# Branch products in another order, one set of weight slots, and a norm in four steps: a hybrid encoder layer

## The chip, the core and the metric

The kernel runs on one core of a Trainium2 chip. The metric is the device time of one execution in microseconds (us), the median of several runs. A core has five engines with a queue each: TensorE (PE in the profile: matrix products, with a separate queue of weight loads, PEld), VectorE (DVE), ScalarE (ACT), GpSimd (POOL) and SyncE (SP), which here issues every DMA. The engines run side by side and wait for one another by semaphores; each works off its own queue in order.

## The reference

One layer over x of 1024 tokens by 1024 features, all in float32. The shift, scale and gate of each of the three sublayers come from a conditioning vector.

```
x += 0.5 * g1 * SwiGLU1(mod1(RMSNorm(x)))                       # first feed-forward, width 2816
h  = mod2(RMSNorm(x))
x += g2 * W_out( sigmoid(gA) * W_A(FoX(h)) + sigmoid(gB) * W_B(DSA(h)) )
x += 0.5 * g3 * SwiGLU2(mod3(RMSNorm(x)))                       # second feed-forward
```

FoX and DSA are two attentions of 8 heads each, 512 features wide; their outputs are the two branches. Each goes through its own matrix (512 by 1024), is multiplied by a sigmoid gate, and the sum of both goes through W_out (1024 by 1024).

## The kernel before

**Arithmetic.** Activations lie with features on the 128 partitions and tokens along the free axis, in two halves of 512 tokens. Every float32 operand is split into a high and a low part (ACT makes the high one by a copy, DVE the low one by a subtraction), and a product is three matmuls: high x high, high x low, low x high. So each weight tile costs one operation on ACT and one on DVE before PE can use it; `wh` and `wl` in the profile are these parts, `wr` and `a` the raw weights as loaded.

**Feed-forwards.** Both use a two-by-two scheme with seven products instead of eight. `Operands` makes the seven right-hand operands from the normalized input: b11, b21 from the first token half, b22, t1, t2, t3, t4 from both halves. `UpPair` does the up products of one pair of feature blocks in 14 steps (seven operands, two matrices); there are 11 pairs. A product is 12 matmuls of 128x512. The first four steps need only the first token half, so the pairs at the head run these first, while the second half is made ready. `UpPair.load1` loads the two raw weights of a pair for each of two matrices (four half tiles), `load2` the other four, `sum32` and `sum14` form weight sums on DVE. `Down` runs seven passes (0 to 6) of 11 steps, each step two splits and 12 matmuls; at the end of a pass DVE adds the four results to the residual.

**Norm between first feed-forward and mixer.** `stats` takes the mean square of a token half (four tiny matmuls against a column of ones, `nacc`, and a reciprocal root in 12 small DVE operations), `norm_spread` broadcasts the factors by four matmuls, and `norm_apply` then makes the mixer's input block by block: DVE multiplies (`nt`), ACT scales and shifts, ACT copies the high part (`h`), DVE subtracts for the low part. For the first token half this is put into pass 5 of `Down`, four blocks at step 6 and four at step 8 (line 2088). For the second half it comes after pass 6. `first(tk)` projects a block of 128 tokens onto 432 columns, in 24 matmuls; it needs only the first half for tk 0 to 3.

**Branches and output.** `Branches.first` (beside the attention) does two of the eight output blocks of the first branch. `Branches.rest` does the others: it goes through the output blocks d two at a time, for each the products of the first and then of the second branch (line 1783), then gates, adds and splits the results. The gated values are `gr`, loaded from DRAM and overwritten. The merged operand m of the first token half goes to the pool h0b, that of the second half ("m" in the profile) to "common". `mixer_out` multiplies by W_out in 16 steps and does beside it the loads of x, the statistics and the first operands of the second feed-forward.

**Slots.** Tiles come from named homes: "h0" and "h1" (16 tiles each), "c" (the pool "common", 52 tiles in the first feed-forward and 41 from the branches on), and "g". In the last stage "g" holds raw weights of the branches, of W_out and of the up pairs; it is the class `Pairs`, which takes over the six tiles of 128x1024 of an older pool, two each under the tags wr, wh and wl, and cuts every one into two halves. A new tile takes the next tag in rotation and has to wait for one of the two buffers of that tag.

**Order.** The kernel doesn't issue instructions as written. `Plan` collects them as tasks in the written order, with a cost for each, and `flush` (line 292) lists them: at each step it takes over all engines the task that can start first, ties going to the one written first, with slots taken from those that have come free. The result is the fixed order of each engine's queue. The first feed-forward up to the mixer's first projection is one plan (to line 2132), and branches, output and second feed-forward are another (line 2280).

Of the kernel before, what the change touches and what calls it, by code (L numbers as in the profile page):

```python
# [9 lines left out]
F32 = mybir.dt.float32  # L10
# [56 lines left out]
class Pairs:  # L67


    def __init__(self, p, tags):  # L70
        self.p, self.tags, self.n, self.rest = p, tags, 0, None
# [73 lines left out]
class LateTile(View):  # L145
# [8 lines left out]
    def real(self):  # L154
        if self.t is None:
            kw = self.kw
            if self.pool.own and kw.get("tag"):
                if self.slot is None:
                    free = self.pool.plan.slots(self)
                    free.sort()  # L160
                    self.slot = free.pop(0)[1]
                    free.append(((free[-1][0] if free else 0.0) + 1.0, self.slot))
                kw = dict(kw, tag=f"{kw['tag']}{self.slot}", bufs=1)
            self.t = self.pool.p.tile(self.full, self.dt, **kw)
        return self.t
# [25 lines left out]
class Plan:  # L191
# [6 lines left out]
    def __init__(self, tc):  # L198
        self.tc, self.on, self.tasks, self.behind = tc, False, [], 0
        self.free = {e: 0.0 for e in self.ENGINES}  # L200
        self.wire, self.done, self.spare, self.window = 0.0, {}, 10, 200
        self.kept, self.wanted = {}, []
# [59 lines left out]
    def close(self):  # L262

        self.on = False
        for x in self.kept.values():
            if x.slot is not None:
                self.slots(x).append((x.end, x.slot))
# [24 lines left out]
    def flush(self, keep=()):  # L292
# [38 lines left out]
        while len(order) < len(tasks):  # L331
# [40 lines left out]
            for x in t.tiles:  # L372
                x.uses -= 1
                x.end = max(getattr(x, "end", 0.0), end)
                if not x.uses and x.slot is not None:
                    self.slots(x).append((x.end, x.slot))
# [994 lines left out]
class Operands:  # L1371
# [37 lines left out]
    def second(self):  # L1409
# [5 lines left out]
        t2, t3 = [], []  # L1415
# [310 lines left out]
class Branches:  # L1726
# [40 lines left out]
    def rest(self, pt1):  # L1767
        k, nc = self.k, self.k.nc
        m = [[None] * 8, [None] * 8]
        for d0 in range(0, 8, 2):  # L1770
            if d0 == 0:
                w = [lambda c, i=i: part8(self.w[i], c) for i in range(2)]
                for hf in range(2):
                    for pr in range(4):
                        t, a, b = k.h_tile(0, F32), t512(k, F32R, "yh"), t512(k, F32R, "yl")
                        nc.sync.dma_start(t, k.d_y[1][pr][:, hf * H:hf * H + H])
                        split(k, a, b, t)
                        self.y[hf].append((a, b))
            else:
                w = [[k.wq.split(k.wq.raw(self.wbr[d0 + i], j, "c" if d0 == 2 else "g")) for j in range(2)] for i in range(2)]  # L1780
                w = [lambda c, i=i, w=w: part4(w[i], c) for i in range(2)]
            ps = {}
            for br in range(d0 == 0, 2):
                for i in range(2):
                    for hf in range(2):
                        ps[br, i, hf] = pt1()
                        self.product(ps[br, i, hf], w[i], br, hf)
            for i in range(2):
                for hf in range(2):
                    sl, t = slice(hf * H, hf * H + H), []  # L1790
                    for br in range(2):
                        if (br, i, hf) in ps:
                            g = t512(k, name="gr")
                            nc.sync.dma_start(g, k.d_gate[br * 8 + d0 + i, :, sl])
                            self.gated(g, ps[br, i, hf])
                            t.append(g)
                        else:
                            t.append(self.t[i][:, sl])
                    nc.vector.tensor_add(t[1], t[1], t[0])
                    a, b = (k.h_tile(0) if hf == 0 else t512(k, F32R, "m") for _ in range(2))  # L1800
                    split(k, a, b, t[1])
                    m[hf][d0 + i] = (a, b)
# [93 lines left out]
def layer(tc, xT, c, pos, ada_w, ada_b, ng, inv, w13a, w2a, w_a, w_f, w_q, w_g, fb, fg, dg, wbr, wout, w13b, w2b, out):  # L1896
    with ExitStack() as es:
# [55 lines left out]
        with ExitStack() as ph:  # L1953
# [134 lines left out]
            steps = {(5, 4): [lambda: stats(0)], (5, 6): [lambda: h0(range(4))], (5, 8): [lambda: h0(range(4, 8))]}  # L2088
# [25 lines left out]

            stats(1)
            rb = norm_spread(k, rms[1], bank)
            first(0)
# [105 lines left out]
        with ExitStack() as ph:  # L2223
# [3 lines left out]
            k.homes = {"h0": (hp[0], "h", 16), "h1": (hp[1], "h", 16), "g": (Pairs(w2, (("wr", 2), ("wh", 2), ("wl", 2))), "g", 12),  # L2227
# [118 lines left out]
```

## Time and profile before

| | |
|---|---|
| median of 3 runs | 2262.19 us (2261.89 to 2266.63) |
| the profiled execution | 2265.69 us |
| its span, first to last instruction | 2264.0 us |
| instructions | 31118 |
| PE busy | 2184.9 us |
| DVE busy | 1800.8 us |
| ACT busy | 1097.6 us |
| mean granted clock of PE | 0.988 |
| DMA packets | 315.89 MB |

Times in the profile are microseconds from the start of the span. Almost every instruction is issued from one line of `flush`, so that all rows bear its number, L386, and groups are told apart by the names of their tiles: `b<-h,wh` is a matmul that writes a bank b of the result memory from operand h with weight wh. Behind a row in the timeline, brackets give the idle time of the engine just before it and what ended it. The granted clock is 1.00 at full rate and 0.50 at half.

### The profile page before, as it was taken

Reading aid. Unit: us, or ns where it says so; the run is one execution under the profiler, and the core shown is the slowest. Engines: PE = TensorE matmul, PEld = TensorE weight load, DVE = VectorE, ACT = ScalarE, POOL = GpSimd, SP = SyncE. Lnnn points to the kernel's source line nnn. Section 1 sums busy time; section 2 is a strip of 40 time slices with the busy share of each in tenths; the row PEclk is TensorE's granted clock in tenths of the full one; section 3 lists DMA queues with packets and bytes.
Section 4 is the critical chain, followed back from the end, with each engine's and each line's share of the span. In section 5 each row is a group of like instructions: output and inputs, shape, how many; then the busy total and the mean of one; then the engine's idle time right before and its main releaser. Section 6 shows DMA issues by size and latency. Waiting matters only on the chain.

```text
span 2264.0 us, 31118 instructions
## 1 busy us (share of the span) xinstructions
PE 2184.9 (97%) x10508; PEld 1802.6 (80%) x10508; DVE 1800.8 (80%) x3387; ACT 1097.6 (48%) x1994; POOL 271.9 (12%) x257
## 2 busy tenths in 40 slices
PE   7999999999999999999899999999999999999999
PEld 5777788787878989987677787787778888888887
DVE  7998987889785488888888877768978877769765
ACT  5432332344463475778777777423533333334443
POOL 0000000000010223222555443000000000000000
PEclk9999999999999999999999999999999999999999
DMA  9234554497321313333332212658123442258520
GB/s 332 84 111 161 170 168 135 149 362 253 112 86 48 120 62 115 117 121 109 122 105 92 72 56 87 239 192 278 61 92 125 145 132 94 94 182 318 167 76 38
DMA packets 186269, 315.89 MB, mean 140 GB/s; under 512 B 27238, under 2 KB 51814, under 8 KB 186108
## 3 DMA queue, kind: packets, MB, share of 16 engines
q1 hardware_dynamic: 186108, 313.89, 41.2%
q8 instruction: 83, 1.36, 0.2%
q14 instruction: 78, 0.64, 0.1%
HBM read 237.53 MB, written 76.28 MB: 139 GB/s over the span
## 4 chain that ended last, share of the span: by engine, by line
PE 44%; DVE 3%; ACT 3%; issue 1%; DMA 1%; SPq 0%; DVEq 0%; ACTq 0%; POOL 0%; POOLq 0%
PE b L386 33%; PE py L386 6%; PE p L386 2%; PE pt L386 2%; ACT pth L386 1%; ACT pr L386 1%; DMA wr<-d_y 0%; DVE wl L386 0%; ACT qs L386 0%; DMA wr<-in_w_g 0%; DVE ptl L386 0%; DMA mraw<-in_ada_w 0%; DVE macc L386 0%; DVE qs L386 0%; DVE xb L386 0%
## 5 line engine op out<-in xcount | busy, mean ns | idle before, releaser
L386 PE MATMUL b<-h,wh 128*128 128x512 f32 x2688 | 851.1, 399 | 15.1 <-ACT wh L386 8.9
L386 PEld LDWEIGHTS b<-h,wh 128*128 128x128 f32 x2688 | 509.1, 190 | 140.6 <-ACT wh L386 13.4
L386 PE MATMUL b<-h,wl 128*128 128x512 f32 x1344 | 529.0, 396 | 2.0 <-DVE wl L386 2.0
L386 ACT ACTIVATE wh<-wr 128x512 fp32r<-128x512 f32 (+2 forms) x366 | 245.3, 678 | 470.4 <-PE b L386 338.4
L386 PEld LDWEIGHTS b<-h,wl 128*128 128x128 f32 x1344 | 255.0, 190 | 63.6 <-DVE wl L386 3.5
L386 DVE TENSOR_TENSOR z<-b,z 128x512 f32<-128x512 f32 x308 | 207.4, 684 | 76.0 <-PE b L386 74.3
L386 PE MATMUL b<-wl,wh 128*128 128x512 f32 x616 | 240.4, 390 | 5.5 <-DVE wl L386 5.5
L386 PE MATMUL b<-wh 128*128 128x512 f32 x616 | 238.7, 390 | 1.9 <-ACT wh L386 1.2
L386 PE MATMUL b<-wh,wl 128*128 128x512 f32 x616 | 239.7, 389 | 0.0
L386 DVE TENSOR_TENSOR wl<-wr,wh 128x512 fp32r<-128x512 f32 x308 | 204.1, 683 | 36.0 <-ACT wh L386 35.9
L386 ACT ACTIVATE wh<-a 128x512 fp32r<-128x512 f32 x132 | 83.3, 631 | 192.6 <-PE b L386 169.0
L386 POOL TENSOR_TENSOR wl<-wr,wh 128x1024 fp32r<-128x1024 f32 (+2 forms) x58 | 123.7, 2137 | 299.3 <-ACT wh L386 299.3
L386 DVE TENSOR_TENSOR wl<-a,wh 128x512 fp32r<-128x512 f32 x132 | 91.4, 692 | 75.4 <-ACT wh L386 75.4
L386 PEld LDWEIGHTS b<-wl,wh 128*128 128x128 f32 x616 | 115.6, 188 | 31.5 <-DVE wl L386 7.5
L386 PEld LDWEIGHTS b<-wh 128*128 128x128 f32 x616 | 115.6, 188 | 27.1 <-ACT wh L386 1.7
L386 PEld LDWEIGHTS b<-wh,wl 128*128 128x128 f32 x616 | 115.5, 188 | 24.1 <-DVE wl L386 0.2
L386 DVE TENSOR_TENSOR z<-z 128x512 f32<-128x512 f32 x176 | 119.5, 691 | 10.9 <-ACT wh L386 0.5
L386 PE MATMUL pj<-wh,h 128*128 128x384 f32 (+1 forms) x512 | 126.4, 325 | 0.1
L386 POOL TENSOR_SCALAR pr<-pr,mn 128x128 f32<-128x128 f32 (+7 forms) x128 | 101.6, 806 | 154.8 <-DVE mn L386 123.2
L386 DVE TENSOR_TENSOR wl<-g,wh 128x512 fp32r<-128x512 f32 x154 | 106.7, 695 | 0.0
L386 PE MATMUL p<-kst,qs 128*128 128x512 f32 (+5 forms) x384 | 104.0, 363 | 1.8 <-DVE qs L386 0.7
L386 PE MATMUL py<-h,wh 128*128 128x512 f32 x288 | 102.5, 409 | 1.6 <-DVE qs L386 1.4
(298 smaller groups left out, 3806.3 us busy)
## 6 DMA issues: line engine op xcount, KB each, us to landing
d_g<-z SPq DMA_DIRECT2D x154, 256.0 KB
g<-d_g SPq DMA_DIRECT2D x154, 256.0 KB
mraw<-in_ada_w SPq DMA_DIRECT2D x144, 256.0 KB
wr<-in_w13a SPq DMA_DIRECT2D x112, 256.0 KB
wr<-in_w13b SPq DMA_DIRECT2D x88, 256.0 KB
wr<-in_w_g SPq DMA_DIRECT2D x32, 512.0 KB
a<-in_w2a SPq DMA_DIRECT2D x44, 256.0 KB
a<-in_w2b SPq DMA_DIRECT2D x44, 256.0 KB
```

Of the source, the lines that this page charges most:

```text
L386: getattr(getattr(self.tc.nc, e), t.op)(*map(real, t.a), **{n: real(v) for n, v in t.kw.items()})
```

## The change

It has four parts.

- `Pairs` no longer rotates over tags. Its six tiles are one set, and a new one takes any that is free. `Plan.merge` joins the lists of free slots, and `Plan.release` gives a slot back to the joint list; these are steps of the planner in Python and issue no instruction.
- `Operands.second`, used in both feed-forwards, keeps two of its sums in place of old tiles of x instead of four new tiles. t1's difference is now made first, with t2; t3's is made just before its conversion; the subtraction for t4 moves behind t1's conversion.
- `Branches.rest` does all remaining products of the first branch (d = 2 to 7, both token halves), keeping the twelve gated results in "common", and then all eight blocks of the second branch. The loads of the second branch's values come after the first block of the first branch. Weights of the first branch go to "c", of the second to "g". The merged operand of the second token half goes to h1.
- The norm of the first token half moves from two steps in pass 5 to four steps of two blocks each in pass 6, and the first projection block is written ahead of the statistics of the second token half.

```diff
@@ class Pairs
-            tag, bufs = self.tags[self.n % len(self.tags)]
-            self.n += 1
-            t = self.p.tile([128, T], dt, tag=tag, name=name, bufs=bufs)
+            t = self.p.tile([128, T], dt, name=name, **self.kw)
@@ class Plan
+    def release(self, x):
+        key, n = self.merged.get(x.key, (x.key, 0))
+        self.done[key].append((x.end, n + x.slot))
+
+    def merge(self, pool, tags):
+        n, to = 0, (pool, "any")
+        self.done[to] = []
+        for tag, bufs in tags:
+            self.done[to] += [(t, n + i) for t, i in self.done.get((pool, tag), [(0.0, i) for i in range(bufs)])]
+            self.merged[pool, tag] = to, n
+            n += bufs
@@ Operands.second
         def sums(c):
-            t3.append(t512(k, name="t3"))
             t2.append(t512(k, name="t2"))
-            self.any.tensor_sub(t3[c], x[c + 4][1], x[c][1])
-            self.any.tensor_add(t2[c], x[c][0], t3[c])
+            self.any.tensor_sub(x[c][0], x[c][1], x[c][0])
+            self.any.tensor_sub(t2[c], x[c + 4][1], x[c][0])
             self.pair("t2", t2[c], self.shift(c + 4), "h1")
...
         for c in range(4):
-            self.pair("t3", t3[c], d[:, c:c + 1], "h1")
+            self.any.tensor_sub(x[c][1], x[c + 4][1], x[c][1])
+            self.pair("t3", x[c][1], d[:, c:c + 1], "h1")
+        yield
+        for c in range(4):
+            self.pair("t1", x[c][0])
         for c in range(4):
             self.any.tensor_sub(x[c + 4][0], x[c + 4][0], t2[c])
-        yield
-        for c in range(4):
-            self.any.tensor_sub(x[c][1], x[c][1], x[c][0])
-            self.pair("t1", x[c][1])
         yield
@@ Branches.rest, the new loops
+        for d in range(2, 8):
+            w = half(d, 0, "c")
+            for hf in range(2):
+                t[d, hf] = gated(0, d, hf, w)
+            if d == 2:
+                for hf in range(2):
+                    for pr in range(4):
+                        y, a, b = k.h_tile(0, F32), t512(k, F32R, "yh"), t512(k, F32R, "yl")
+                        nc.sync.dma_start(y, k.d_y[1][pr][:, hf * H:hf * H + H])
+                        split(k, a, b, y)
+                        self.y[hf].append((a, b))
+        for d in range(8):
+            w = (lambda c: part8(self.w[d], c)) if d < 2 else half(d, 1, "g")
+            for hf in range(2):
+                g = gated(1, d, hf, w)
+                nc.vector.tensor_add(g, g, t[d, hf])
+                a, b = k.h_tile(hf), k.h_tile(hf)
+                split(k, a, b, g)
+                m[hf][d] = (a, b)
@@ layer
-            steps = {(5, 4): [lambda: stats(0)], (5, 6): [lambda: h0(range(4))], (5, 8): [lambda: h0(range(4, 8))]}
+            steps = {(5, 4): [lambda: stats(0)]}
+            steps.update({(6, c): [lambda c=c: h0(range(c, c + 2))] for c in range(0, 8, 2)})
...
+            first(0)
             stats(1)
             rb = norm_spread(k, rms[1], bank)
-            first(0)
             first(1)
```

Here `gated(br, d, hf, w)` does one product, loads its gate and multiplies; `half(d, br, home)` loads and splits the half tile of weights of one branch.

More of the change, by code (lines that the diff above doesn't have):

```diff
@@ L67, with __init__ @@
 class Pairs:
-    def __init__(self, p, tags):
-        self.p, self.tags, self.n, self.rest = p, tags, 0, None
+    def __init__(self, plan, p, tags):
+        self.p, self.rest = p, None
+        self.kw = dict(tag="any", bufs=sum(n for _, n in tags), names=[f"{t}{i}" for t, n in tags for i in range(n)])
+        plan.merge(id(p), tags)
     def tile(self, shape, dt, name, **_):
         if self.rest is None:
-            tag, bufs = self.tags[self.n % len(self.tags)]
-            self.n += 1
-            t = self.p.tile([128, T], dt, tag=tag, name=name, bufs=bufs)
+            t = self.p.tile([128, T], dt, name=name, **self.kw)
             self.rest = t[:, H:T]
@@ L162, in real @@
                     free.append(((free[-1][0] if free else 0.0) + 1.0, self.slot))
-                kw = dict(kw, tag=f"{kw['tag']}{self.slot}", bufs=1)
+                kw = dict(kw, tag=kw["names"][self.slot] if "names" in kw else f"{kw['tag']}{self.slot}", bufs=1)
+                kw.pop("names", None)
             self.t = self.pool.p.tile(self.full, self.dt, **kw)
@@ L266, in close @@
             if x.slot is not None:
-                self.slots(x).append((x.end, x.slot))
+                self.release(x)
         self.kept = {}
@@ L375, in flush @@
                 if not x.uses and x.slot is not None:
-                    self.slots(x).append((x.end, x.slot))
+                    self.release(x)
                     self.kept.pop(id(x), None)
@@ L1769, in rest, with gated @@
         m = [[None] * 8, [None] * 8]
-        for d0 in range(0, 8, 2):
-            if d0 == 0:
-                w = [lambda c, i=i: part8(self.w[i], c) for i in range(2)]
+        t = {(i, hf): self.t[i][:, hf * H:hf * H + H] for i in range(2) for hf in range(2)}
+        def gated(br, d, hf, w):
+            ps = pt1()
+            self.product(ps, w, br, hf)
+            g = t512(k, name="gr")
+            nc.sync.dma_start(g, k.d_gate[br * 8 + d, :, hf * H:hf * H + H])
+            self.gated(g, ps)
+            return g
@@ L1782, in rest @@
[L1782 to L1802, printed above, removed]
+        for d in range(8):
[6 more added lines that the diff above has]
+                m[hf][d] = (a, b)
```

15 lines of the change are left out of this document (6 added, 9 removed).

## The prediction

> **What bounds the kernel now.** I read the page first, then a table of stages, then in each stage TensorE's idle times with the names of what ended them.
>
> ```profile
> PE 2184.9 (97%) x10508; PEld 1802.6 (80%) x10508; DVE 1800.8 (80%) x3387; ACT 1097.6 (48%) x1994; POOL 271.9 (12%) x257
> ```
>
> TensorE (PE) is busy for 2184.9 of 2264.0 us, and no matmul is added or dropped by this change. So all that can be won is idle time of PE, 79.1 us, and time that it spends at a lower clock. The table of stages (columns: busy us of PE, of its weight load, of DVE, ACT, POOL, then granted clock, DMA share, GB/s) shows where that is:
>
> ```profile
> 0.00:350.00 350.00, 327.85 (x1381) 257.85 (x1382) 311.46 (x542) 127.61 (x214) 1.19 (x8) 0.97 0.50 170
> 350.00:725.00 375.00, 366.14 (x1604) 298.51 (x1603) 303.28 (x501) 165.22 (x287) 9.87 (x8) 0.99 0.49 167
> 725.00:1430.00 705.00, 670.52 (x3974) 581.06 (x3973) 554.30 (x1324) 503.30 (x991) 260.89 (x241) 0.99 0.30 99
> 1430.00:1607.00 177.00, 175.08 (x765) 140.41 (x764) 136.46 (x227) 64.81 (x108) 0.00 (x0) 1.00 0.67 227
> 1607.00:1700.00 93.00, 86.30 (x358) 68.68 (x357) 78.60 (x135) 36.96 (x63) 0.00 (x0) 0.94 0.21 73
> ```
>
> The rows are: first FFN's up products, its down passes with the norm into the mixer, projections and attention, branches with output projection, and the head of the second FFN. The change edits code in all but the third. The stage of the branches holds only 1.9 us of idle time. The two that can give something are the norm (640 to 714) and the head of the second FFN (1607 to 1668). PE's timeline has these waits there (start, duration, instruction, and in brackets the idle time before it and who ended it):
>
> ```profile
> 664.23 0.50 PE L386 MATMUL b<-wl,wh 128*128 128x512 f32 x1 [0.22 <-DVE wl L386]
> 669.78 0.47 PE L386 MATMUL b<-wh 128*128 128x512 f32 x1 [0.72 <-DVE nt L386]
> 679.95 0.50 PE L386 MATMUL b<-wl,wh 128*128 128x512 f32 x1 [3.18 <-DVE wl L386]
> 706.15 1.86 PE L386 MATMUL b<-ones_col,nacc 128*128 128x1 f32 x8 [2.33 <-DVE nacc L386]
> ...
> 1640.33 0.51 PE L386 MATMUL b<-h,wl 128*128 128x512 f32 x1 [1.96 <-DVE wl L386]
> 1655.64 1.22 PE L386 MATMUL b<-h,wh 128*128 128x512 f32 x2 [3.46 <-ACT wh L386]
> 1665.06 0.51 PE L386 MATMUL b<-h,wh 128*128 128x512 f32 x1 [0.39 <-DVE z L386]
> 1666.45 0.50 PE L386 MATMUL b<-h,wh 128*128 128x512 f32 x1 [0.89 <-DVE h L386]
> ```
>
> Some waits are followed by a time at half clock. The table in steps of 2 us (same columns; the number behind PE's busy time also counts matmuls cut by the edges):
>
> ```profile
> 678.00:680.00 2.00, 0.05 (x1) 0.05 (x1) 2.00 (x5) 1.23 (x3) 0.00 (x0) 1.00 0.87 316
> ...
> 706.00:708.00 2.00, 1.85 (x9) 1.85 (x9) 0.10 (x1) 0.00 (x0) 0.00 (x0) 0.50 0.12 47
> 712.00:714.00 2.00, 2.00 (x13) 1.93 (x12) 0.00 (x0) 0.53 (x1) 0.00 (x0) 0.82 0.02 6
> ...
> 1640.00:1642.00 2.00, 1.67 (x6) 1.34 (x7) 2.00 (x5) 0.06 (x1) 0.00 (x0) 0.79 0.00 0
> 1642.00:1644.00 2.00, 2.00 (x6) 1.62 (x5) 1.28 (x3) 0.08 (x1) 0.00 (x0) 0.50 0.00 0
> 1644.00:1646.00 2.00, 2.00 (x9) 1.53 (x9) 1.65 (x3) 1.59 (x3) 0.00 (x0) 0.86 0.00 0
> ...
> 1656.00:1658.00 2.00, 2.00 (x6) 1.47 (x6) 1.60 (x3) 0.28 (x1) 0.00 (x0) 0.50 0.94 303
> 1660.00:1662.00 2.00, 2.00 (x7) 1.55 (x6) 0.60 (x1) 1.26 (x3) 0.00 (x0) 0.59 0.00 0
> ```
>
> Time lost there is two us times one minus the clock: 2 x (0.21 + 0.50 + 0.14) = 1.7 us after the wait of 1.96; 2 x (0.50 + 0.50 + 0.41) = 2.8 after that of 3.46 (1658 to 1660 is at 0.50 too); about 3.4 after that of 2.33 (706 to 712 at 0.50, then 0.82). The wait of 3.18 has 1.00 behind it and cost only itself.
>
> **Sum of what is there to win.** Norm: 0.22 + 0.72 + 3.18 + 2.33 = 6.45, and 3.4 of clock: 9.85 us. Head of the second FFN: 1.96 + 3.46 + 0.39 + 0.89 = 6.70, and 1.7 + 2.8: 11.2 us.
>
> **One set of weight slots.** The six half-pairs of "g" were handed out by rotation over wr, wh, wl with two buffers each. Counting the loads in the order of the code (4 tiles in the branches, then output weights, pair 0 between the 14th and the 15th of them, pairs 1 and 2 after), pair 0's second half, pair 1's first and pair 2's second are tiles 19, 22 and 25: all three fall on wh. So pair 2's second half must wait until pair 0 has used its own for the last time, while a slot of wl stands empty. The trace agrees: up to 1610 there are 18 loads of these weights where pairs 0 to 2 ask for 20 (8, 8 and 4), and the chain of waits then shows the missing two, released by the last weight split of pair 0:
>
> ```profile
> wr<-in_w13b SPq DMA_DIRECT2D x18, 256.0 KB
> ...
> 1651.15 0.61 DVE wl L386
> ...
> 1651.78 3.07 DMA wr<-in_w13b
> ...
> 1654.95 0.64 ACT wh L386
> ...
> 1655.64 8.58 PE b L386 x24
> ```
>
> With any free slot the load joins those of about 1600, and two products of 12 matmuls move ahead of the wait at 1638. Two undisturbed stretches give their length (branch products, of the same form, then down passes):
>
> ```profile
> 1475.00:1500.00 25.00, 25.00 (x109) 20.28 (x109) 13.27 (x21) 5.07 (x8) 0.00 (x0) 1.00 0.25 85
> 2100.00:2125.00 25.00, 25.00 (x112) 20.71 (x111) 19.02 (x31) 10.38 (x18) 0.00 (x0) 1.00 0.68 232
> ```
>
> 24 matmuls at 25 us / 109 are 5.5 us. The wait of 3.46 and its 2.8 of clock go. The 1.96 goes too if DVE's weight split at 1639.6 comes at most 5.5 us later: what the two products bring to DVE ahead of it is two splits, an add and a product, 4 x 0.6 = 2.4 us, so it does, with 1.1 us to spare (1639.6 + 2.4 against 1638.3 + 5.5, less 0.7 for the split itself). What is late next is DVE, which holds the operands of the second half:
>
> ```profile
> 1637.18 2.49 DVE L386 TENSOR_TENSOR xb<-xb,t 128x512 f32<-128x512 f32 x4
> 1639.59 0.69 DVE L386 TENSOR_TENSOR wl<-s,wh 128x512 fp32r<-128x512 f32 x1
> ...
> 1647.46 3.09 DVE L386 TENSOR_TENSOR wl<-wr,wh 128x512 fp32r<-128x512 f32 x5
> ```
>
> So I keep a remainder: at best 0, at worst all that DVE ended (1.96 + 0.39 + 0.89 + 1.7 = 4.9), and take 2.5, the middle. Gain 11.2 - 2.5 = 8.7 us.
>
> **Operands made in place.** Before and after, each block of four has 8 subtractions or additions for the sums, 4 for t4 and 4 for the last operand, all of 0.6 us by the rows above (2.49 for four, 3.09 for five). None is added; four for t3 now stand ahead of its conversion and four for t4 go behind t1. Four slots of "common" are freed. Zero in both FFNs, unless the re-planning below says otherwise.
>
> **Norm in four steps.** Now it runs in bursts of four blocks inside pass 5 of 0 to 6 (654 and 667), in which DVE stands still behind ACT:
>
> ```profile
> 654.02 2.47 DVE L386 TENSOR_TENSOR nt<-xc,b 128x512 f32<-128x512 f32 x4
> ...
> 659.05 0.69 DVE L386 TENSOR_TENSOR h<-nt,h 128x512 fp32r<-128x512 f32 x1 [0.68 <-ACT h L386]
> ```
>
> A burst takes DVE 7 us (654.0 to 661.1), so the weight splits come late, and the second burst meets the additions between passes: hence 0.22, 0.72 and 3.18. After, pass 5 has none of this and enters pass 6 with its splits ahead. Pass 6 asks of DVE 22 splits and 16 norm operations of 0.60, 8 additions of 0.66 and 4 square sums of 0.60: 30.5 us, beside 132 matmuls of 25 us / 112 = 29.5 us on PE. That is tight: with four stalls of 0.68 DVE is 33.2 us, 3.7 over. Against it stand the splits done ahead, up to 4 of 11 steps (8 slots, two each), 10.7 us of PE's work. Bounds: 0, and 3.7 with a half clock like 1.7 to 2.8, so about 6; I take 2.5, since an earlier pass end with the same 8 additions shows 0.96:
>
> ```profile
> 610.36 0.50 PE L386 MATMUL b<-wl,wh 128*128 128x512 f32 x1 [0.96 <-DVE wl L386]
> ...
> 713.72 21.61 PE L386 MATMUL b<-wa,h 128*128 128x432 f32 x108
> ```
>
> The 12 matmuls of the first mixer block that filled a hole at 674 go behind the pass: no cost, PE does them either way.
>
> **First mixer block ahead of the statistics.** The four tiny matmuls waited 2.33 us for DVE's last square, with 24 ready matmuls queued behind them on PE. Now those 24 (21.61 / 108 = 0.20 us each in the last row, 4.8 us) cover it; the statistics then come 2.5 us later, and the rest of their chain (7.6 us, from 706.15 to 713.72) has 72 matmuls, 14.4 us, over it. 2.33 and 3.4 go. Norm: 9.85 - 2.5 = 7.35 us.
>
> **Branches.** 28 products, 28 gate loads, 12 weight loads, 8 loads of the second branch's values: the same counts on PE, DVE, ACT and SP. What moves is order. The first product now needs a loaded and split weight instead of the second branch's values:
>
> ```profile
> 1435.02 0.50 PE L386 MATMUL b<-yl,wh 128*128 128x512 f32 x1 [0.91 <-DVE yl L386]
> ...
> 1431.77 0.45 SPq L386 DMA_DIRECT2D d_y<-yt  x1
> ```
>
> That 0.91 goes if the weight is loaded early. If SP issues it only after the last store of the attention at 1431.77, it lands 3.07 later, and with ACT's 0.64 PE waits from 1433.5 to 1435.5, 2 us, and perhaps 1.7 of clock: -0.9 to +2.8. I take 0. The twelve gated tiles fill slots that the merged operand leaves ("m", 16 tiles, goes to h1); these are free once the first branch is done.
>
> **The sum.** 8.7 + 7.35 = 16.05 us off the profiled execution of 2265.69 us, 3.5 above the median of 2262.19. I take the same 16 us off the median: **2246.0 us**.
>
> **The clock rule.** By the Trainium skill (TensorE: Matmul & The Clock Gate, "What's actually happening") the clock halves after at least one idle window of about 3.4 us, and the windows run freely. The rows differ: half clock stands behind waits of 1.96 and 2.33 us, not behind 3.18, so the measurement decides on the length; the free phase fits both. What follows for time is rival D.
>
> **The rivals.**
> A. DVE can't carry the norm in pass 6: the remainder is the 6 us of the bound and 3.5, half a burst, by which the last blocks hold up the first mixer block; 9.5 instead of 2.5. For: 30.5 against 29.5 us. Against: splits ahead. 2253.0 us.
> B. The change doesn't do what it says in the second FFN: the load comes no earlier, since the planner sends it behind others, or DVE ends the same wait: 8.7 less, 2254.7. Against: the slot count above.
> C. A and B: 2261.7, no change.
> D. Half clock falls by phase: with all times moved, two of the remaining waits, such as 3.82 at 227 (below), get it or lose it, 2.8 us each: 2251.6, or 2240.4.
> E. Slower: the order on every engine is a list plan, and the whole first FFN is one plan, so the freed slots shift its loads. DVE is busy for 311 of its first 350 us, and there is a stall already:
>
> ```profile
> 226.94 1.65 PE L386 MATMUL b<-h,wh 128*128 128x512 f32 x3 [3.82 <-ACT wh L386]
> 228.00:230.00 2.00, 2.00 (x6) 1.61 (x5) 2.00 (x4) 0.00 (x0) 0.00 (x0) 0.50 0.67 202
> ```
>
> Such a stall costs 3.82 and, as above, 2.8 of clock: 6.6 us. It decides from the fourth on, which takes 26.4 for the 16 won: **2272.6 us**. Against: DVE's work there is the same.
>
> **Chances.** Forecast 0.45, A 0.15, B 0.10, C 0.04, D 0.08, E 0.18, of which 0.04 are two or three stalls only, no change. A measurement of this kernel can tell about 0.2%, 4.5 us, from nothing: faster 0.78, same 0.08, slower 0.14. Range: all 21 us, 0.9 at the branches and 4 of D's clock give 2236; on the other side it takes in A and B and reaches to C, 2261.
>
> **What would show it.** Right: 20 loads of the up weights before 1610, no DMA in PE's chain there, no idle time before the statistics' matmuls, and clock 1.00 in both places. Wrong: waits for wl inside pass 6 every two steps (A), the two products still behind pair 0 (B), new waits before 300 us (E).

## The result and the profile after

The changed kernel takes 2254.46 us (median of 6 runs, 2250.57 to 2257.17) beside 2266.61 us (median of 6, 2261.89 to 2269.36) of the kernel before: ratio 0.9943, 95% interval 0.9928 to 0.9958, 12 us faster. Measured a second time, with the last four runs below, it was 0.9921 (0.9906 to 0.9936), 17 us. The profiled executions are 2265.69 and 2255.36 us. The forecast of 16 us less lies between the two measurements; the forecast time of 2246.0 us is 8.5 below the result.

The page's first line and the table of stages of the changed kernel, with the same columns and edges as before (its rows bear the line number L400):

```profile
PE 2180.4 (97%) x10508; PEld 1799.2 (80%) x10508; DVE 1798.8 (80%) x3387; ACT 1099.3 (49%) x1994; POOL 273.7 (12%) x257
```

```profile
0.00:350.00 350.00, 325.60 (x1370) 255.43 (x1371) 310.18 (x541) 126.88 (x213) 1.20 (x8) 0.98 0.50 170
350.00:725.00 375.00, 371.96 (x1641) 304.13 (x1641) 304.37 (x506) 168.22 (x290) 10.65 (x8) 1.00 0.50 168
725.00:1430.00 705.00, 669.13 (x3964) 578.77 (x3962) 554.49 (x1325) 501.91 (x988) 261.86 (x241) 0.99 0.30 96
1430.00:1607.00 177.00, 172.10 (x741) 137.92 (x742) 140.38 (x234) 64.56 (x106) 0.00 (x0) 0.99 0.74 247
1607.00:1700.00 93.00, 92.88 (x409) 75.27 (x408) 82.99 (x142) 42.85 (x70) 0.00 (x0) 1.00 0.17 60
```

The work on each engine is the same. In the second row PE's idle time fell from 8.9 to 3.0 us, in the last from 6.7 to 0.1, and its clock there rose from 0.94 to 1.00. In the fourth row it went the other way, 1.9 us idle became 4.9, and in the first 22.2 became 24.4. PE's timeline names what stands behind this: first the end of the norm, where the statistics' matmuls (`ones_col,nacc`) now stand between mixer blocks and wait for nothing, then the two new waits, one at the start of the branches and one at the output projection.

```profile
703.77 2.56 PE L400 MATMUL b<-wa,h 128*128 128x432 f32 x12
706.21 1.05 PE L400 MATMUL b<-ones_col,nacc 128*128 128x1 f32 x8
707.12 3.02 PE L400 MATMUL b<-wa,h 128*128 128x432 f32 x14
...
1432.40 1.20 PE L400 MATMUL b<-h,wh 128*128 128x512 f32 x4 [2.61 <-ACT wh L400]
...
1533.53 0.50 PE L400 MATMUL b<-h,wl 128*128 128x512 f32 x1 [2.50 <-DVE wl L400]
```

Of the eight waits that the prediction listed, 0.2 us is left in the norm and 0.1 at the head of the second feed-forward. In the chain of waits that head is two stretches of PE with a weight split of DVE between them, and no transfer stands in it; and among the DMA issues between 1430 and 1610 there are 23 loads of its up weights, 18 before:

```profile
1599.89 49.17 PE b L400 x219
...
1650.37 0.61 DVE wl L400
...
1651.03 19.16 PE b L400 x82
```

```profile
wr<-in_w13b SPq DMA_DIRECT2D x23, 256.0 KB, 4.7
```

The wait of 2.61 us is the one whose length the prediction worked out for the branches. In the chain of waits a store (SPq) is followed by the load of the first weight, ACT's split and PE; SP's own timeline shows why the load was not earlier, five stores of the attention that wait for the data which DVE makes for them (in both lists: start, duration):

```profile
1427.94 0.45 SPq L400
1428.48 3.16 DMA wr<-in_wbr
1431.72 0.64 ACT wh L400
```

```profile
1412.86 15.53 SPq L400 DMA_DIRECT2D d_y<-yt  x5
1428.48 0.54 SPq L400 DMA_DIRECT2D wr<-in_wbr  x1
```

**One ruler for all runs.** Two profiled executions differ by some us in places that no edit touches, so whole times hide the parts. Four points are easy to find in each trace: the wait of 0.96 at the end of a down pass, the first product of the mixer (`pj`), the last of the attention (`py`), the first of the second feed-forward's down passes. In the changed kernel:

```profile
615.15 0.50 PE L400 MATMUL b<-wl,wh 128*128 128x512 f32 x1 [0.96 <-DVE wl L400]
...
741.21 0.33 PE L400 MATMUL pj<-wh,h 128*128 128x384 f32 x1
...
1429.40 0.39 PE L400 MATMUL py<-h,wl 128*128 128x512 f32 x1
...
2038.81 0.39 PE L400 MATMUL b<-wh 128*128 128x512 f32 x1
```

The starts of these rows cut a trace in four. A is the first feed-forward to its fourth down pass, B the rest of it with the norm and the mixer's first projection, C projections and attention, D branches, output and the up products of the second feed-forward. Behind D come the down passes of the second feed-forward, 210.5 us from their first matmul to the start of their last in every trace. Lengths in us of all profiled executions, named after the parts that each kernel has; the last column is the time lost to half clock within C, two us times one minus the clock over rows of 2 us:

| kernel | A | B | C | D | lost in C |
|---|---|---|---|---|---|
| before | 610.4 | 136.2 | 686.7 | 615.9 | 6.8 |
| slots | 614.6 | 137.7 | 687.4 | 604.1 | 6.9 |
| norm | 614.1 | 126.1 | 687.9 | 615.6 | 8.5 |
| branches | 612.5 | 137.6 | 689.8 | 617.3 | 8.5 |
| operands | 615.2 | 137.9 | 688.8 | 613.6 | 6.8 |
| slots, norm | 612.3 | 126.0 | 686.2 | 605.0 | 5.1 |
| slots, norm, branches | 612.0 | 126.0 | 688.6 | 606.8 | 6.8 |
| slots, norm, operands | 614.3 | 126.1 | 688.4 | 604.7 | 6.8 |
| all (after) | 615.2 | 126.1 | 688.2 | 609.4 | 6.8 |
| all, old start of the branches | 611.7 | 126.1 | 690.4 | 605.2 | 8.5 |
| all, second profile | 613.1 | 126.1 | 692.7 | 607.9 | 12.0 |
| slots, norm, second profile | 613.5 | 126.1 | 686.4 | 604.9 | 5.1 |
| slots, second profile | 613.7 | 136.1 | 689.2 | 604.4 | 8.5 |
| norm, second profile | 609.3 | 126.1 | 688.1 | 615.4 | 8.5 |

### The profile page after: what moved, and what is told of

Its sections match the earlier page's. It is cut to its first block, busy times and chain, and to the rows that moved or that the text cites. A ratio compares the mean times of both kernels' runs of the same rounds, so it can differ in the third digit from the quotient of the medians.

```text
span 2253.6 us, 31135 instructions
## 1 busy us (share of the span) xinstructions
PE 2180.4 (97%) x10508; PEld 1799.2 (80%) x10508; DVE 1798.8 (80%) x3387; ACT 1099.3 (49%) x1994; POOL 273.7 (12%) x257
## 3 DMA queue, kind: packets, MB, share of 16 engines
q8 instruction: 83, 1.36, 0.3%
## 4 chain that ended last, share of the span: by engine, by line
PE 44%; DVE 3%; ACT 2%; DMA 1%; issue 1%; SPq 0%; ACTq 0%; POOL 0%; DVEq 0%; POOLq 0%
PE b L400 33%; PE py L400 7%; PE p L400 2%; PE pt L400 2%; ACT pth L400 1%; DVE gr L400 1%; DVE macc L400 1%; ACT pr L400 1%; ACT qs L400 0%; DMA wr<-in_w_g 0%; DMA wr<-in_wbr 0%; DVE ptl L400 0%; DMA wr<-in_wout 0%; DVE h L400 0%; DVE wl L400 0%
## 5 line engine op out<-in xcount | busy, mean ns | idle before, releaser
L400 PE MATMUL b<-h,wh 128*128 128x512 f32 x2816 | 887.5, 397 | 13.4 <-ACT wh L400 11.4
L400 PEld LDWEIGHTS b<-h,wh 128*128 128x128 f32 x2816 | 530.9, 189 | 143.6 <-ACT wh L400 16.0
L400 PE MATMUL b<-h,wl 128*128 128x512 f32 x1408 | 554.0, 396 | 4.6 <-DVE wl L400 4.5
L400 ACT ACTIVATE wh<-wr 128x512 fp32r<-128x512 f32 (+2 forms) x366 | 245.1, 678 | 448.3 <-PE b L400 315.1
L400 PEld LDWEIGHTS b<-h,wl 128*128 128x128 f32 x1408 | 266.2, 189 | 69.5 <-DVE wl L400 6.8
L400 DVE TENSOR_TENSOR z<-b,z 128x512 f32<-128x512 f32 x308 | 207.9, 687 | 76.6 <-PE b L400 75.0
L400 PE MATMUL b<-wl,wh 128*128 128x512 f32 x616 | 240.6, 391 | 2.1 <-DVE wl L400 1.9
L400 PE MATMUL b<-wh,wl 128*128 128x512 f32 x616 | 240.5, 391 | 0.0
L400 PE MATMUL b<-wh 128*128 128x512 f32 x616 | 238.0, 390 | 1.8 <-ACT wh L400 1.8
L400 DVE TENSOR_TENSOR wl<-wr,wh 128x512 fp32r<-128x512 f32 x308 | 203.8, 686 | 31.1 <-ACT wh L400 31.0
L400 ACT ACTIVATE wh<-a 128x512 fp32r<-128x512 f32 x132 | 83.4, 632 | 190.1 <-PE b L400 169.5
L400 POOL TENSOR_TENSOR wl<-wr,wh 128x1024 fp32r<-128x1024 f32 (+2 forms) x58 | 123.8, 2139 | 307.0 <-ACT wh L400 303.2
L400 DVE TENSOR_TENSOR wl<-a,wh 128x512 fp32r<-128x512 f32 x132 | 91.4, 692 | 74.8 <-ACT wh L400 74.8
L400 PEld LDWEIGHTS b<-wl,wh 128*128 128x128 f32 x616 | 115.9, 188 | 27.4 <-DVE wl L400 3.2
L400 PEld LDWEIGHTS b<-wh 128*128 128x128 f32 x616 | 116.0, 188 | 26.7 <-ACT wh L400 2.3
L400 PEld LDWEIGHTS b<-wh,wl 128*128 128x128 f32 x616 | 116.0, 189 | 24.3 <-DVE wl L400 0.4
L400 DVE TENSOR_TENSOR z<-z 128x512 f32<-128x512 f32 x176 | 119.5, 691 | 9.9 <-ACT z L400 0.3
L400 PE MATMUL pj<-wh,h 128*128 128x384 f32 (+1 forms) x512 | 126.5, 325 | 0.1
L400 POOL TENSOR_SCALAR pr<-pr,mn 128x128 f32<-128x128 f32 (+7 forms) x128 | 102.5, 814 | 154.9 <-DVE mn L400 124.8
L400 DVE TENSOR_TENSOR wl<-g,wh 128x512 fp32r<-128x512 f32 x154 | 106.6, 694 | 0.3 <-ACT wh L400 0.3
L400 PE MATMUL p<-kst,qs 128*128 128x512 f32 (+5 forms) x384 | 104.0, 363 | 1.9 <-DVE qs L400 0.7
L400 ACT ACTIVATE z<-z 128x512 f32<-128x512 f32 x88 | 55.5, 630 | 101.0 <-DVE z L400 99.7
```

Source lines behind the costliest of these rows:

```text
L400: getattr(getattr(self.tc.nc, e), t.op)(*map(real, t.a), **{n: real(v) for n, v in t.kw.items()})
```

## The experiments

**The theory** is that of the prediction: slots and norm each gain at their own place, the other two parts cost little. **The rival** is that the net of 12 us hides a larger gain and a loss made by the branches or the operands, or that the parts work on each other. First each part alone, all on one chip. Rows of PE in the fences of this section are from PE's timeline of the kernel just named.

**Slots alone.** The new `Pairs`, and in the plan `merge` and `release`; all else as before.

```diff
-            tag, bufs = self.tags[self.n % len(self.tags)]
-            t = self.p.tile([128, T], dt, tag=tag, name=name, bufs=bufs)
+            t = self.p.tile([128, T], dt, name=name, **self.kw)
```

> The kernel before with only the one set of weight slots. Theory (each part acts in its own stage, and the parts add up): the late load of the second half of pair 2 goes, with it the waits of 1.96 and 3.46 us and the half clock behind both at the head of the second feed-forward; 8 to 11 us faster, nothing before 1600 us changed. Rival (the gain there needs the slots of the pool common that the other parts free): DVE still ends a wait of 2 us or more near 1640, at most 5 us faster.

Measured: 2257.59 us (12 runs) beside 2266.08, ratio 0.9960 (0.9949 to 0.9972). Of the four waits at the head of the second feed-forward one is left:

```profile
1655.88 0.51 PE L400 MATMUL b<-h,wl 128*128 128x512 f32 x1 [0.48 <-DVE wl L400]
```

D is 604.1 and 604.4 us in its two profiles, against 615.9, 615.6 and 615.4 in the three profiles with the old slots, branches and operands. With the slots and the old branches and operands (four profiles) the mean is 604.6: a gain of 11.0 us. The wait of 2 us or more near 1640 that the rival asked for isn't there.

**Norm alone.** Four steps in pass 6, and the first block ahead of the statistics.

```diff
-            steps = {(5, 4): [lambda: stats(0)], (5, 6): [lambda: h0(range(4))], (5, 8): [lambda: h0(range(4, 8))]}
+            steps = {(5, 4): [lambda: stats(0)]}
+            steps.update({(6, c): [lambda c=c: h0(range(c, c + 2))] for c in range(0, 8, 2)})
...
+            first(0)
             stats(1)
             rb = norm_spread(k, rms[1], bank)
-            first(0)
```

> The kernel before with only the norm in four steps of pass 6 and the first projection block ahead of the statistics. Theory: the four waits between 664 and 706 (6.45 us) and 3.4 us at half clock go; 8 to 10 us faster, and the first 600 us are as before. Rival (the up products of the first feed-forward are in the same plan, and it is this edit that shifts them): some of the 4.8 us that the changed kernel loses before 615 us appear here, so 4 to 6 us faster.

Measured: 2259.62 us (10 runs) beside 2266.08, ratio 0.9970 (0.9959 to 0.9982). No wait is left in the norm; the head of the second feed-forward keeps its four, of which the two long ones are

```profile
1634.48 0.50 PE L386 MATMUL b<-h,wl 128*128 128x512 f32 x1 [1.97 <-DVE wl L386]
1650.08 1.22 PE L386 MATMUL b<-h,wh 128*128 128x512 f32 x2 [3.75 <-ACT wh L386]
```

B is 126.0 or 126.1 us in all nine profiles with this part, 136.1 to 137.9 in the five without it (mean 137.1): 11.0 us gained. The spread on one side only is the half clock, 3.4 us in two of the five and 5.1 in three. With its mean of 4.4 the waits of 6.45 us make 10.9. By the rival, part of the loss before 615 us should appear here; A is 3.7 us longer than before in this profile and 1.1 shorter in the second one, so nothing shows it. The whole time gives less than the stretch, 6.5 us (4.1 to 9.3 by the interval), and in the second measurement 11.5; why it gave less the first time stays open.

**Branches alone.**

```diff
-        for d0 in range(0, 8, 2):
+        for d in range(2, 8):
+            w = half(d, 0, "c")
...
+        for d in range(8):
+            w = (lambda c: part8(self.w[d], c)) if d < 2 else half(d, 1, "g")
```

> The kernel before with only the new order of the branches. Theory: a wait of 2.6 us at the first branch product (its weight is issued behind the last store of the attention) in place of 0.9, and a wait of 2.5 us with 1.7 of half clock early in the output projection, where loads of the modulation weights, let in by freed slots, hold DVE; together 5 to 6 us slower, unless more free slots shorten the head of the second feed-forward. Rival (the second wait comes from the other parts): only 2 us slower.

Measured: 2271.12 us (12 runs) beside 2266.08, ratio 1.0023 (1.0013 to 1.0034), slower. The wait of 0.91 at the start became 2.48, and a second one is new at the output projection:

```profile
1442.64 2.07 PE L386 MATMUL b<-h,wh 128*128 128x512 f32 x4 [2.48 <-ACT wh L386]
...
1544.51 0.50 PE L386 MATMUL b<-h,wl 128*128 128x512 f32 x1 [1.42 <-DVE wl L386]
```

With 1.7 us of half clock behind the first this is 2.48 - 0.91 + 1.7 + 1.42 = 4.7 us. Its profile has only 1.7 us of half clock at the head of the second feed-forward, where the kernel before has 5.1, so that D is only 1.4 us longer than in that profile.

**Operands alone.**

```diff
-            self.any.tensor_sub(t3[c], x[c + 4][1], x[c][1])
-            self.any.tensor_add(t2[c], x[c][0], t3[c])
+            self.any.tensor_sub(x[c][0], x[c][1], x[c][0])
+            self.any.tensor_sub(t2[c], x[c + 4][1], x[c][0])
```

> The kernel before with only the operands made in place. Theory: the four freed slots change the plan of the first feed-forward's up products, waits around 100 us grow from 3.8 to 5.8 and one more of 1.8 near 557; 3 to 5 us slower by 615 us, nothing in the second feed-forward. Rival (those differences are not from the operands): within 1 us of the kernel before at 615 us.

Measured: 2269.98 us (12 runs) beside 2266.08, ratio 1.0018 (1.0008 to 1.0029). The plan of both feed-forwards changes. At the head of the second one the waits are other ones, with 3.4 us of half clock:

```profile
1647.29 0.50 PE L386 MATMUL b<-h,wl 128*128 128x512 f32 x1 [0.77 <-DVE wl L386]
1661.93 1.22 PE L386 MATMUL b<-h,wh 128*128 128x512 f32 x2 [4.29 <-ACT wh L386]
1672.40 0.50 PE L386 MATMUL b<-h,wh 128*128 128x512 f32 x1 [2.02 <-DVE h L386]
```

That is 7.1 us for 6.7 before. In the first feed-forward the wait near 102 of 2.73 and the one near 107 of 1.04 became 0.94, 2.03, 0.76 and 1.98, so 5.7 us for 3.8. A of the five profiles with this part is 613.9 in the mean, of the nine without it 612.5, in a spread of 5. So 1.4 to 1.9 us lost in the first feed-forward have a place; for the rest of 3.9 none can be shown, since D is shorter than before.

The four ratios together give -0.29%, half of the whole change's -0.57%. The next four were to show whether the parts work on each other.

**Slots and norm**, without the other two (the diffs of the first and the second run):

> The slots and the norm together, branches and operands as before. Theory 1 (the parts add up): the two gains alone were 0.9960 and 0.9970, so 0.9930, 2250 us beside 2266 of the kernel before, faster than the whole change. Theory 2 (the two bad parts cost nothing in company, since the merged slots cover what they delay): the same ratio as the whole change, 0.9943, 2253. In the trace by both: no waits over 1 us at the end of the norm and at the head of the second feed-forward; the waits of the first feed-forward as before (2.7, 1.0, 1.1, 0.6, 3.8, 1.2); branches begin behind 0.9, and no wait of 2.5 near 1530.

Measured: 2246.01 us (5 runs) beside 2269.31, ratio 0.9902 (0.9886 to 0.9919), below both theories, on another chip than the single parts. Its waits are those expected, but for the one near 554, which is 2.17 us instead of 1.2; it is 1.2 to 2.84 in the fourteen traces, whatever the parts.

**Slots, norm and branches** (and the third's):

> As the run with slots and norm, and the new order of the branches. Theory 1 (the parts add up): 0.0023 above the run without it, about 5 us: 2255. From the traces I would give it 2.6 - 0.9 at the start of the branches and 2.5 + 1.7 of clock at the start of the output projection, 5.9 us. Theory 2: no difference to the run without it.

Measured: 2249.15 us (5 runs), ratio 0.9911 (0.9895 to 0.9926).

```profile
1429.48 1.20 PE L400 MATMUL b<-h,wh 128*128 128x512 f32 x4 [2.41 <-ACT wh L400]
...
1530.02 0.50 PE L400 MATMUL b<-h,wl 128*128 128x512 f32 x1 [0.47 <-DVE wl L400]
```

So the loss at the start stays in company, and the late split at the output projection is there without the operands. The wait for it is short because PE lost 1.7 us to half clock behind the first wait and came to it that much later (more on this at the last runs). D is 2.2 us longer than the mean without the branches and the difference of the medians is 3.1, between the two theories.

**Slots, norm and operands** (first, second and fourth):

> As the run with slots and norm, and the operands made in place. Theory 1: 0.0018 above the run without it, about 4 us: 2254. Theory 2: what the operands alone lost stood at the head of the second feed-forward (waits of 0.8, 4.3 and 2.0), which the merged slots take away, so no difference, and in the first feed-forward their waits are 7.5 us as against 10.4 of before: 0 to 3 us faster.

Measured: 2248.09 us (4 runs), ratio 0.9904 (0.9889 to 0.9919), beside 0.9902 without the operands: 2.1 us by the medians. A is 2.0 longer too (614.3 for 612.3), but 1.7 of that is half clock. These few runs can't tell it from nothing.

**All, with the old start of the branches**: the second branch's first two products come first, with the weights that lie in memory already, then the first branch.

```diff
...
+        for d in range(2):
+            for hf in range(2):
+                g = gated(1, d, hf, lambda c: part8(self.w[d], c))
+                nc.vector.tensor_add(t[d, hf], g, t[d, hf])
         for d in range(2, 8):
             w = half(d, 0, "c")
...
-                g = gated(1, d, hf, w)
-                nc.vector.tensor_add(g, g, t[d, hf])
+                g = t[d, hf]
+                if w:
+                    g = gated(1, d, hf, w)
+                    nc.vector.tensor_add(g, g, t[d, hf])
```

> The changed kernel, except that the branches begin as before with the second branch's first two products, whose weights are in memory already; the rest of the first branch comes after them. Theory 1 (the new start costs: a weight whose load waits behind the last store): the wait of 2.6 becomes 0.9 and nothing else moves: 1.7 us below the changed kernel, 2253. If the late splits at 1533 come from the order of the branches too, these 2.5 and 1.7 of clock go as well: 2249. Theory 2 (what the order costs lies in the loads that bunch because slots are free earlier): the wait of 2.5 at the output projection stays.

Measured: 2249.11 us (4 runs), ratio 0.9910 (0.9894 to 0.9926).

```profile
1429.96 0.50 PE L400 MATMUL b<-yl,wh 128*128 128x512 f32 x1 [0.91 <-DVE yl L400]
...
1527.19 0.50 PE L400 MATMUL b<-h,wl 128*128 128x512 f32 x1 [0.99 <-DVE wl L400]
```

The start is that of before, and D is 605.2, within 0.6 us of the kernels with the old branches. So with the old start the new order costs almost nothing in the trace: 1.7 us of wait are gone at the start, and the late split at the output projection, with no half clock ahead of it in either kernel, costs 0.99 where it cost 2.50. The medians, 3.1 us above slots and norm with some 2 for the operands in it, are too coarse to add to that.

**On one chip: all, slots and norm, and each of these alone, again.** Here the edits are those above.

> The whole change again, beside its two good parts on the same chip; so far they were measured on other chips than the whole. Theory 1 (the parts add up, and a ratio differs from chip to chip by some 0.3%): the whole is about 0.001 above slots and norm together, since on one chip the branches cost 0.0009 there and the operands 0.0002. Theory 2 (the whole costs more than its parts, by the late splits at the output projection, 2.5 and 1.7 us, which neither the branches nor the operands show without the other): 0.003 above slots and norm, and these 4 us are in its trace again at about 1530.

> Slots and norm again, on the same chip as the whole and as each of the two alone. Theory 1: the product of the two ratios of this chip, within 0.0015. Theory 2 (the two help each other): at least 0.002 below the product, as the runs on two chips had it, 0.9902 against 0.9930.

> The slots alone again, on the chip of the other three. From its trace, 11.8 us less from the end of the attention to the down passes of the second feed-forward: 0.9948. Measured on another chip: 0.9960.

> The norm alone again, on the chip of the other three. From its trace, 10.1 us less from the middle of the first feed-forward's down passes to the mixer's first product: 0.9955. Measured on another chip: 0.9970.

Measured, beside 2266.94 of before: slots 2257.43 us (6 runs), 0.9955 (0.9939 to 0.9971); norm 2255.49 (5 runs), 0.9945 (0.9931 to 0.9959); both 2247.29 (4 runs), 0.9907 (0.9892 to 0.9922); all 2250.36 (6 runs), 0.9921 (0.9906 to 0.9936). The product of the two single ratios is 0.9900, and 0.9907 was measured: they add up. That the parts help each other falls; the figures of the first four runs and the fifth came from two chips. The whole is 3.1 us above slots and norm by the medians, 4.2 by the means (95% interval of these few runs 0.7 to 7.7). Its trace, in the second profile of the same program:

```profile
1434.86 1.29 PE L400 MATMUL b<-h,wh 128*128 128x512 f32 x4 [2.62 <-ACT wh L400]
...
1535.88 0.50 PE L400 MATMUL b<-h,wl 128*128 128x512 f32 x1 [0.94 <-DVE wl L400]
```

and in its chain of waits

```profile
1535.23 0.61 DVE wl L400
```

The wait at the output projection is 0.94 where it was 2.50, so it is not a fixed 4 us of the whole change either. The split is as late as before: DVE ends it 101.0 us after the start of the first branch product here (1535.23 + 0.61 - 1434.86), and 101.1 us in the first profile (1532.88 + 0.61 - 1432.40, a row shown in the next section). What moved is PE: here it lost 1.7 us to half clock behind the first wait, there nothing. It came to the split that much later, with the same 424 matmuls between, and waited less. Time lost ahead of a wait is taken off that wait; the two don't add up.

Slots and norm alone are faster than the kernel before (0.9902 and 0.9907), and on this chip faster than the whole change too.

## Why the prediction was right

**The direction, the size of the gain and both places** were right. By the stretches of the ruler: B 11.0 less, D 11.0 less by the slots, D 4.0 more by the rest of the change (608.7, mean of the whole's two profiles, less 604.6), A perhaps 1.4 more. That is 16.6 us less; forecast were 16.05. That the two are so close is luck: both gains were put too low by 2.3 and 3.65, and the losses of 5.4 that cancel this were put at 0.

- **Slots: 8.7 forecast, 11.0 measured.** The account of the slots was right: the loads come early (23 before 1610, where 20 were asked for as a sign), no transfer stands in the chain. The term that was mis-sized is the remainder of 2.5, "the middle" of 0 to 4.9: at most 0.5 us is left (0.48 with the slots alone, 0.12 in the whole), so the two products moved ahead cover DVE as the working above that remainder had it. The half clock was too low as well: the row 1654 to 1656, at 0.70, belongs to it, so that 3.4 us and not 2.8 stand behind the wait of 3.46.
- **Norm: 7.35 forecast, 11.0 measured.** Again a remainder of 2.5 stood for DVE in pass 6, asked for 30.5 us there. The stretch of pass 6 in the changed kernel shows 25.7 us in 42 operations and PE busy without a gap but 0.2:

```profile
674.00:704.00 30.00, 29.78 (x132) 24.30 (x132) 25.70 (x42) 20.31 (x34) 0.00 (x0) 1.00 0.16 59
```

  Asked for were 50: 22 weight splits, 16 operations of the norm, 8 additions and 4 square sums. The groups of the same stretch (count, then busy us and mean ns) show 17 splits:

```profile
L400 DVE TENSOR_TENSOR wl<-g,wh 128x512 fp32r<-128x512 f32 x9 | 6.2, 685 | 0.0
L400 DVE TENSOR_TENSOR wl<-a,wh 128x512 fp32r<-128x512 f32 x8 | 5.5, 685 | 0.0
```

  With them go 16 operations of the norm, 4 additions and 5 square sums. So five splits were done ahead; that is what the prediction set against its remainder ("splits done ahead, up to 4 of 11 steps"), five splits of the eight it allowed for. And of the eight additions at the end of pass 5, seven start before 674; the other three in the stretch are of pass 6 itself. DVE didn't hold up PE, and the remainder was 0.2 us. The half clock was put at 3.4 and is 4.4 in the mean. The two halves of this part, four steps and block ahead of the statistics, were not tried apart.
- **Branches: 0 forecast, about 4 us lost in the whole.** The step "I take 0" failed. The prediction held the mechanism and its length (2 us; 2.4 to 2.6 were measured), and I took the 0 between its bounds of -0.9 and 2.8. The weight was not loaded early: it is the first load of a new plan, and in SP's queue it stood behind the stores until the attention's end. The wait at the output projection was not seen at all. There SP's timeline of the changed kernel has 14 loads of `mraw` in a row, of before 7, ahead of the loads that follow:

```profile
1502.65 9.37 SPq L400 DMA_DIRECT2D mraw<-in_ada_w  x14
```

```profile
1512.12 4.61 SPq L386 DMA_DIRECT2D mraw<-in_ada_w  x7
```

  They move earlier, probably because slots of "common" are free earlier. DVE's operations on them (`macc`), each behind its load, stand in DVE's queue ahead of the weight split that PE needs; the chain of waits of the changed kernel leads there:

```profile
1527.20 4.12 DMA mraw<-in_ada_w
1531.35 0.76 DVE macc L400
1532.13 0.75 DVE macc L400
1532.88 0.61 DVE wl L400
```

  The bunch and the wait go with the branches: the branches alone, with slots and norm, and with the old start have 14, 14 and 15 in a row and waits of 1.42, 0.47 and 0.99, while slots and norm have 7 and no wait there. That the freed slots make the bunch, and the bunch the wait, is argued from these rows and not tried.
- **Operands: 0 forecast.** Alone 1.0018, in company 0.0002 more. Some 1.4 to 2 us seem lost in the first feed-forward, where the re-planning that the prediction set aside with "unless" took place; alone the loss was larger, and why stays open.
- **The rivals of the prediction.** A (DVE holds up pass 6) and B (slots don't help) fall, with C. E asked for four stalls of 6.6 in the first feed-forward; its waits were re-planned, but for 1.9 us more and not 26. D (half clock by phase) is no rival but goes on in every run, in both directions (below).
- **The time.** Of the 8.5 us by which 2246.0 is too low, 4.4 are the base: 2262.19 was the median of three runs, with six it is 2266.61, and the profiled 2265.69 pointed there. Another 3.9 are 16.05 less the 12.15 of this measurement, and 0.1 is rounding; in the second measurement the gain was 16.6.

## What to carry to other kernels

A rotation over buffers of equal size makes a load wait for one of them while another stands empty; count which tile falls on which buffer before anything else. When an order is turned round, look at its first operation: does its operand lie in memory when the stage begins, and what stands ahead of its load in the queue? And measure parts alone and together on one chip: of four edits that went as one, two carried the gain, and without the other two the kernel was 3 to 4 us faster still (interval 0.7 to 7.7).

## What the runs showed of the hardware

**Half clock by phase.** The same program, the same wait, two executions. After the 2.61 us in the first profile of the whole change the clock is 1.00; after 2.62 us in the second one it is halved:

```profile
1434.00:1436.00 2.00, 2.00 (x10) 1.60 (x9) 1.04 (x2) 1.31 (x3) 0.00 (x0) 1.00 0.99 319
```

```profile
1434.00:1436.00 2.00, 1.14 (x5) 0.91 (x6) 0.69 (x1) 0.63 (x1) 0.00 (x0) 0.95 0.89 303
1436.00:1438.00 2.00, 2.00 (x6) 1.60 (x5) 0.43 (x1) 1.02 (x2) 0.00 (x0) 0.50 0.84 294
1438.00:1440.00 2.00, 2.00 (x7) 1.55 (x6) 0.98 (x3) 1.19 (x3) 0.00 (x0) 0.69 1.03 371
```

The loss is 2 x (0.05 + 0.50 + 0.31) = 1.7 us, half of 3.4, and in all fourteen traces each loss is 1.7 us or two or three times that, but for the one that the end of the span cuts. It was seen behind a wait of 1.68 us (near 556, slots alone), even behind 1.08 us (near 27 in every trace, right after matmuls of a single column), and missed behind the 3.18 of the kernel before. By the Trainium skill (TensorE: Matmul & The Clock Gate, "What's actually happening") the clock halves after at least one idle window of about 3.4 us; the 3.4 agrees with how long the half clock lasts here, but these waits, shorter than a window, had it too.

The traces show what the phase is. In each of them all half clocks begin a whole number of steps of 3.41 us apart, and what counts is how a wait falls on these steps. In the kernel before a half clock begins at 705.90; eight steps earlier, at 678.59, is the edge of a step, and it cuts the wait of 3.18 (676.77 to 679.95) into 1.82 and 1.36 us: no half clock. In the first profile of the changed kernel one begins at 1534.03, and the shorter wait of 2.50 (1531.03 to 1533.53) lies whole in the step that ends there:

```profile
1534.00:1536.00 2.00, 2.00 (x7) 1.52 (x6) 1.93 (x5) 0.07 (x1) 0.00 (x0) 0.51 0.78 212
```

Counted over all steps at full clock after the first 30 us of the fourteen traces, half clock followed every step in which PE was busy for less than 0.45 of the time, and none in which it was busy for more than 0.67.

**It makes most of the spread between executions.** Stage C is the same program in all kernels as far as its work goes, and is 686.2 to 692.7 us long. The time lost there to half clock goes from 5.1 to 12.0 us in the same traces (correlation 0.88); without it C is 679.3 to 682.0. The 33 executions of the kernel before, taken beside the single parts, agree: the five with a mean granted clock of 0.992 took 2263.6 us in the mean, the six at 0.988 took 2269.7. At one place, the longest and one of the shorter traces of C (all, second profile; slots and norm):

```profile
1074.00:1076.00 2.00, 2.00 (x8) 1.19 (x6) 0.75 (x5) 1.89 (x4) 2.00 (x3) 0.50 0.42 158
1076.00:1078.00 2.00, 1.30 (x5) 0.98 (x5) 1.94 (x6) 1.95 (x7) 2.00 (x1) 0.50 0.84 241
1078.00:1080.00 2.00, 2.00 (x8) 1.70 (x7) 1.35 (x3) 1.98 (x6) 0.04 (x1) 0.50 0.87 255
1080.00:1082.00 2.00, 2.00 (x10) 1.40 (x10) 1.25 (x3) 1.24 (x4) 0.00 (x0) 0.79 0.07 20
```

```profile
1066.00:1068.00 2.00, 1.12 (x6) 1.16 (x6) 0.00 (x0) 0.00 (x0) 1.92 (x3) 0.67 1.01 388
1068.00:1070.00 2.00, 2.00 (x11) 1.60 (x11) 0.96 (x5) 1.89 (x4) 2.00 (x3) 0.50 0.42 163
1070.00:1072.00 2.00, 1.68 (x11) 1.17 (x11) 1.94 (x6) 1.95 (x7) 2.00 (x1) 0.98 0.28 77
```

In the first it lasts two steps of 3.41 us, in the second one. In the norm, waits of 6.45 us therefore cost their length and, in the mean over five traces, about two thirds as much again, 4.4 us. The wait of 0.96 at the end of a down pass, by contrast, has no half clock behind it in any of the fourteen.
